# A two-layer decoder trunk on one core: later weight spreads, row pools opened amid the gate tiles, seven banks

## The chip, the cores and the metric

The kernel runs on one core of a Trainium2 chip. The time is device microseconds of one execution, and the median of several executions is compared. TensorE (PE) does the matmuls, VectorE (DVE), ScalarE (ACT) and GpSimd (POOL) the elementwise work, and SyncE (SP) issues the DMAs in order, so what stands behind a waiting DMA in SP's queue waits too.

## The reference

The program is a trunk of two layers on 1024 tokens of 1024 columns, all in float32. Each layer is a token mixer with a gate, an output projection, a DeepNorm layer norm, and a gated addition of a projected side input:

```python
# layer 0, mixer A: three dilated groups, merged by softmax denominators
h = x @ w_in
for gi, (window, dil) in enumerate(A_GROUPS):          # (128,1) (512,4) (2048,16)
    q, k, v = ...; q, k = apply_rope(q), apply_rope(k)
    o, lse = banded_attention(strided(q), strided(k), strided(v), window // dil)
o = sum_g softmax_g(lse) * o_g
mix = (o * silu(z)) @ w_out                            # z: the last 1024 columns of h
# layer 1, mixer B: 16 query heads on 2 key/value heads, window 128, one sink logit per head
o, _ = banded_attention(q, k, v, B_WINDOW - 1, sinks)
mix = (o * silu(z)) @ w_out
# after each mixer
x = layer_norm(alpha * x + mix)
x = x + sigmoid(x @ Wg_i) * (p[i] @ Wp_i)
```

## The kernel before

The tokens lie in eight row tiles of 128. Weights are taken in blocks of 512 output columns (2 MB of float32, 33 blocks in all). Each block and each activation is split into a float16 pair, hi and lo, and one tile times one block (`lin`, lines 270 to 272) is 24 matmuls of 128x512: hi by hi, hi by lo and lo by hi for eight slices of the inner dimension. One PSUM bank holds the result.

**A weight block** passes ten steps of a generator (class `Block`): four row-max reduces on VectorE (`wpm`, line 108), a 128x128 diagonal of the maxima on VectorE (`mdd`, line 228), which one matmul with a matrix of ones (`s<-mdd,ones`, line 235, "the spread") brings to all partitions so that VectorE can make a power of two of the largest; then four split steps (lines 131 and 132: ACT makes hi, VectorE lo). The raw block lies in one of two buffers (`wraw`); block i + 2 is loaded once block i is split, by four DMAs on SP's queue (line 102). A split waits until the block that held its slot is released. `progress` and `prepare` advance this generator by a number of steps per tile of `lin` work: `W_STEPS` 1.6 in general.

**Layer A**: for two halves of the heads and three groups, a value block and two query/key blocks with rope; the attention is worked off in units (scores, mask and max on VectorE, exps on ACT, a hi/lo split, a transposing DMA to `pT`, value matmuls, `st` to `scr` in DRAM), a few units behind the `lin` tiles. A merge reads `scr` as `gt` and writes `oa`. **Layer B**: a block of keys and values, two query blocks, and units that end in `mu`, stored to `ob`.

**The gate and the rows**: two blocks of gate columns. `z_tile` makes silu of one tile (`zt`, `zu`) and stores it to `za` or `zb`. `rows(n)` loads a merged row tile (`ot`) and its gate (`og`), multiplies them on POOL, splits them and transposes them to `ogT`. `norm(n)` multiplies `ogT` by the two output blocks ("whl" and "wo"), adds the residual row on VectorE (`y`, line 920), takes the statistics (line 921), a reciprocal square root (POOL's pow, line 1003), normalizes (line 927) and transposes `xgT`. `gate` multiplies `xgT` by the two side-gate blocks ("whl" and "wg"), with tanh on ACT. Where code of several stages is open, a scheduler orders each engine's instructions; the pools below set which memory is free when.

Before, `z_block` runs all of gate half 0 and one tile of half 1, then `drain` finishes every attention unit and merge; only then are the pools of the rows (`tp`, `pw`) opened. `mixed` then does the other seven tiles of half 1 with five weight steps each, and `rows` for the last four tiles of these; the other four rows are made within norm.

Of the kernel before, what the change touches and what calls it, by code (L numbers as in the profile page):

```python
# [20 lines left out]
P = 128  # L21
S = 1024
D = 1024
# [57 lines left out]
W_OP = 2  # L81
N_WAKE = 8
Z_AHEAD = 1
ROWS_AHEAD = 4
# [4 lines left out]
class Block:  # L89
# [6 lines left out]
    def load(self):  # L96
        k = self.k
        self.n = NK * self.cols
        self.raw = k.raw.tile([P, NK * 512], F32, tag="wraw", name="wraw")
        q = self.n // 4  # L100
        for c in range(4):
            k.nc.sync.dma_start(self.raw[:, c * q:(c + 1) * q], self.src[:, c * q:(c + 1) * q])

    def maxima(self):
# [7 lines left out]
        yield True  # L112
        e = k.max_spread(diag)
# [25 lines left out]
class Trunk:  # L139
    def __init__(self, ctx, tc, a):  # L140
# [13 lines left out]
        self.uid = 0  # L154
# [25 lines left out]
        self.mhalf = self.const.tile([P, 1], F32, name="mhalf")  # L180
        nc.gpsimd.memset(self.mhalf, -0.5)
# [7 lines left out]
    def rope_tables(self, order):  # L189

        t = self.const.tile([P, N_ROPE], F32, name="rope", tag="rope", bufs=2)
# [124 lines left out]
    def drain(self):  # L316
        due, self.due = self.due, []
        for e in due:
            e[1]()
        while self.units or any(self.pipe):  # L320
            self.unit_step()
        self.merge_every = 1
        while self.merges or self.merging:
            self.merge_step()

# [9 lines left out]
    def rope_out(self, ps, nq, nk, n, dst):  # L335
# [6 lines left out]
        t2 = w.tile([P, 512], F32, tag="t2", name="t2")  # L342
# [8 lines left out]
        hl = w.tile([P, 12, P], F16, tag="hl", name="hl", bufs=3)  # L351
# [18 lines left out]
    def scores(self, qa, kas, mask, cs, ncs, sums, nbias, floor, pool_lo):  # L370
# [31 lines left out]
        nc.sync.dma_start(ptf, pf[:, :8 * nk], transpose=True)  # L402
# [188 lines left out]
    def weight_steps(self):  # L591
# [4 lines left out]
        for i in range(len(b)):  # L596
            yield from b[i].split()
            if i + 2 < len(b):
                b[i + 2].load()
            if i + 1 < len(b):  # L600
                yield from b[i + 1].maxima()

    def next_block(self):
        b = self.blocks[self.bi]
        self.bi += 1
        while not b.done:
            assert next(self.steps)
        return b
# [13 lines left out]
    def layer_a(self):  # L622
# [15 lines left out]
        for pair in range(2):  # L638
            for g in (1, 2, 0):
                if pair and g == 0:  # L640
                    self.merge_every = 1
                self.rope_tables(g)
# [4 lines left out]
                for n in range(NT):  # L647
                    ps = self.ps_lin.tile([P, 512], F32, tag="lin", name="lin")
                    self.lin(ps, blk, *self.stat_a(g, n), 0, 512)
                    self.v_out(ps.rearrange("p (s c) -> p s c", s=2), vh[:, pick, n, :], vl[:, pick, n, :])  # L650
# [19 lines left out]
        self.z_block(self.invx, lambda n: self.stat_a(0, n))  # L670
        self.drain()
# [15 lines left out]
    def unit_a(self, q, g, n, qk, vh, vl, cs, ncs, cv, scr):  # L687
# [4 lines left out]
        def stats():  # L692
            st = at.tile([P, 4 * HD + 8], F32, tag="st", name="st", bufs=len(self.pipe) + 1)
# [21 lines left out]
    def z_rows(self, pool, ps, c):  # L715
# [4 lines left out]
        u = pool.tile([P, 512], F32, tag="t2", name="zu")  # L720
# [4 lines left out]
    def z_tile(self, pool, n, half):  # L725
        ps = self.ps_lin.tile([P, 512], F32, tag="lin", name="lin")
        self.lin(ps, self.w_z, *self.z_stat(n), 0, 512)
        self.nc.sync.dma_start(self.z_dr[n][:, 512 * half:512 * half + 512], self.z_rows(pool, ps, self.cz))

    def z_block(self, invx, stat):  # L730

        self.z_stat = stat
        self.upt = 2.0
        for half in range(2):
            self.w_z = self.next_block()
            self.cz = self.prod(invx, self.w_z.inv, 0.5, "cz")
            for n in range(Z_AHEAD if half else NT):
                self.z_tile(self.work, n, half)
                self.progress()
            if half == 0:  # L740
                self.w_z.released = True

    def merge(self, n, pair, scr):

        nc, at, sp = self.nc, self.att, self.small
# [44 lines left out]
    def layer_b(self, xT, invx):  # L790
# [4 lines left out]
        self.bufs = 3  # L795
        self.rope_tables(0)
# [7 lines left out]
        for n in range(NT):  # L804
# [4 lines left out]
            self.progress()  # L809
# [23 lines left out]
        self.z_block(invx, lambda n: self.stat_t(xT, n))  # L833
        self.drain()
# [35 lines left out]
    def transpose_rows(self, src, s, dst, i, name):  # L870
# [6 lines left out]
        nc.sync.dma_start(t.rearrange("p a k c -> p (a k) c"), hl.rearrange("p a c -> p (a c)"), transpose=True)  # L877
        dst[i] = t

    def mixed(self, l, xres, gate_pool):  # L880
# [4 lines left out]
        g_b = pw.tile([P, D], F32, tag="g_b", name="g_b", bufs=1)  # L885
        b_b = pw.tile([P, D], F32, tag="b_b", name="b_b", bufs=1)
        nc.sync.dma_start(g_b, a["lng"][l].partition_broadcast(P))
        nc.sync.dma_start(b_b, a["lnb"][l].partition_broadcast(P))
# [3 lines left out]
        w_o, cw = [], []  # L892
# [17 lines left out]
        def norm(n):  # L910
            y = pw.tile([P, D], F32, tag="row", name="y", bufs=6)
            nc.sync.dma_start(y, xres(n))
            sc = sp.tile([P, 2], F32, tag="osc", name="osc")
            st = sp.tile([P, 2, 6], F32, tag="bst", name="bst")
            for hf in range(2):
                sl = slice(512 * hf, 512 * hf + 512)
                nc.vector.tensor_mul(sc[:, hf:hf + 1], ris[n], cw[hf])
                ps = self.ps_lin.tile([P, 512], F32, tag="lin", name="lin")
# [13 lines left out]

        done = 0
        for n in range(Z_AHEAD, NT):
            self.z_tile(self.work, n, 1)
            self.tick()
            self.prepare(5)
            if n >= NT - ROWS_AHEAD:
                rows(done)
                done += 1  # L940
        self.w_z.released = True
        for i in range(2):
            b = self.next_block()
            c = self.keep(1, "cw")
            nc.vector.tensor_scalar(c, b.inv, 1.0 / ALPHA, None, op0=ALU.mult)
            w_o.append(b)
            cw.append(c)
        for n in range(NT):
# [4 lines left out]
            if n == 1:  # L953
                wg = gate_pool()
        for b in w_o:
            b.released = True
        return xgT, xg_dr, wg

    def gate(self, l, xgT, xg_dr, last):
# [8 lines left out]
        for n in range(NT):  # L968
# [5 lines left out]
            for c0, c1 in ((0, 512), (512, 768), (768, 1024)) if end else ((0, 512), (512, 1024)):  # L974
                hf, sl, w = c0 // 512, slice(c0, c1), c1 - c0
                ps = self.ps_lin.tile([P, 512], F32, tag="lin", name="lin")[:, :w]
                self.lin(ps, w_g[hf], *self.stat_t(xgT, n), c0 % 512, w)
                t = pw.tile([P, 512], F32, tag=("g_b", "b_b")[hf], name="gth", bufs=1)[:, :w]
# [168 lines left out]
```

## Time and profile before

| | us |
|---|---|
| median of 3 runs (1661.18 to 1664.79) | 1662.65 |
| the profiled execution | 1663.47 |
| its span | 1661.6 |
| TensorE busy | 1587.1 |
| VectorE busy | 1082.3 |
| ScalarE busy | 923.1 |
| GpSimd busy | 673.5 |

By the trace, layer A's attention ends near 975 us, its second gate half begins near 1006, norm near 1047 and the side gate near 1128; layer B's attention lasts from about 1277 to 1462, its norm begins at 1490. A busy time is a mean over all of these stages; where TensorE was idle or ran at a lower clock is read stage by stage.

### The profile page before, as it was taken

The page shows a single profiled execution, that of the slowest core. Times are in us where ns is not written, and L with a number is a line of the kernel's source. Part 1 is how long each engine was busy: PE and PEld are TensorE (multiplying, and loading weights), DVE is VectorE, ACT ScalarE, POOL GpSimd, SP SyncE. Part 2 cuts the span into 40 slices and gives each one's busy share as a digit, 9 for nine tenths or more (in the row PEclk, how much of TensorE's full clock was granted, in tenths as well). Part 3 has the DMA queues.
Part 4 walks back from the last instruction along what each step waited for, and adds up shares of the span by engine and source line. Part 5 has one row for each costly group of instructions (what it writes and reads, how often), then busy time and mean ns, then how long its engine had stood idle before and what let it go on. Part 6 is the DMA issues. An engine that isn't in the chain of part 4 may idle for free. (4 is left out here: it accounts for less than half of the span.)

```text
span 1661.6 us, 29030 instructions
## 1 busy us (share of the span) xinstructions
PE 1587.1 (96%) x10579; PEld 882.0 (53%) x10579; DVE 1082.3 (65%) x2617; ACT 923.1 (56%) x2050; POOL 673.5 (41%) x481
## 2 busy tenths in 40 slices
PE   9899999999999799999999988889999998999998
PEld 3455676654555456766555543334455555544444
DVE  6756665655666876556566567877347988678731
ACT  4526665674765477656657843533334888754321
POOL 0205524432564666154235553452323552225331
PEclk9999999999999899999999999999999999999999
DMA  9617766774887777567558996989975898998963
GB/s 364 247 61 162 169 157 137 159 166 112 160 166 203 212 166 157 133 152 162 143 127 183 187 232 218 329 216 261 250 183 110 160 206 171 189 299 215 260 197 107
DMA packets 543792, 311.02 MB, mean 187 GB/s; under 512 B 473120, under 2 KB 494240, under 8 KB 543392
## 3 DMA queue, kind: packets, MB, share of 16 engines
q1 hardware_dynamic: 543648, 309.16, 75.2%
q8 instruction: 83, 1.36, 0.3%
q14 instruction: 61, 0.50, 0.1%
HBM read 137.78 MB, written 54.92 MB: 116 GB/s over the span
## 5 line engine op out<-in xcount | busy, mean ns | idle before, releaser
L270 PE MATMUL lin<-whl,xhl 128*128 128x512 f16 x1280 | 488.5, 382 | 0.0
L272 PE MATMUL lin<-whl,xhl 128*128 128x512 f16 x1280 | 488.3, 382 | 0.0
L271 PE MATMUL lin<-whl,xhl 128*128 128x512 f16 x1280 | 488.0, 381 | 0.0
L399 POOL TENSOR_TENSOR phl<-sm,phl 128x1024 f16<-128x1024 f32 (+1 forms) x88 | 155.6, 1768 | 233.7 <-ACT phl L397 212.9
L349 POOL TENSOR_TENSOR t<-t,t 128x512 f32<-128x512 f32 (+1 forms) x120 | 153.4, 1278 | 235.5 <-DVE t L348 219.0
L108 DVE TENSOR_REDUCE wpm<-wraw 128x1 f32<-128x1024 f32 (+1 forms) x132 | 157.1, 1198 | 99.3 <-DMA wraw<-in_wa_dram 59.1
L272 PEld LDWEIGHTS <-xhl 128*128 128x128 f16 x1280 | 149.3, 117 | 127.1 <-issue 3.2
L270 PEld LDWEIGHTS <-xhl 128*128 128x128 f16 x1280 | 149.3, 117 | 119.0 <-issue 2.8
L271 PEld LDWEIGHTS <-xhl 128*128 128x128 f16 x1280 | 149.7, 117 | 116.6 <-issue 3.3
L393 ACT ACTIVATE sm<-sm,st,cs 128x128 f32<-128x128 f32 (+1 forms) x384 | 203.6, 532 | 3.3
L356 POOL TENSOR_TENSOR hl<-t,hl 128x512 f16<-128x512 f32 (+1 forms) x120 | 143.5, 1196 | 133.4 <-ACT hl L355 133.4
L387 DVE CUSTOM_DVE_ANT_0 sm<-s,tab 128x256 f32<-128x256 f32 (+1 forms) x512 | 157.1, 358 | 34.3 <-PE s L383 25.8
L132 DVE SCALAR_TENSOR_TENSOR whl<-wraw,s,whl 128x1024 f16<-128x1024 f32 (+1 forms) x116 | 168.6, 1504 | 10.9 <-ACT whl L131 10.9
L355 ACT ACTIVATE hl<-t 128x512 f16<-128x512 f32 (+1 forms) x120 | 72.3, 602 | 123.1 <-POOL t L349 121.6
L345 DVE TENSOR_TENSOR t<-lin,rope 128x512 f32<-128x512 f32 (+1 forms) x120 | 78.9, 658 | 84.3 <-PE lin L272 59.7
L131 ACT ACTIVATE whl<-wraw,s 128x1024 f16<-128x1024 f32 (+1 forms) x116 | 121.8, 1123 | 7.0 <-DVE s L210 7.0
L271 PE MATMUL lin<-whl,x2T 128*128 128x512 f16 (+1 forms) x320 | 115.0, 359 | 0.0
L270 PE MATMUL lin<-whl,x2T 128*128 128x512 f16 (+1 forms) x320 | 115.0, 359 | 0.0
L272 PE MATMUL lin<-whl,x2T 128*128 128x512 f16 (+1 forms) x320 | 115.0, 359 | 0.0
L397 ACT ACTIVATE phl<-sm 128x1024 f16<-128x1024 f32 (+1 forms) x128 | 110.2, 861 | 1.2
L359 ACT ACTIVATE hl<-hl 128x512 f16<-128x512 f16 (+1 forms) x104 | 63.2, 608 | 54.2 <-POOL hl L356 54.0
L383 PE MATMUL s<-qk 128*128 128x128 f16 x1120 | 81.8, 221 | 8.1 <-DMA qk<-hl 8.1
(190 smaller groups left out, 2897.3 us busy)
## 6 DMA issues: line engine op xcount, KB each, us to landing
wraw<-in_wa_dram SPq DMA_DIRECT2D x56, 512.0 KB, 5.8
scr<-st SPq DMA_DIRECT2D x96, 132.0 KB, 2.3
gt<-scr SPq DMA_DIRECT2D x48, 264.0 KB, 3.4
wraw<-in_wav_dram SPq DMA_DIRECT2D x24, 512.0 KB, 6.1
prh<-pro SPq DMA_DIRECT2D x32, 256.0 KB, 4.6
wraw<-in_wg_dram SPq DMA_DIRECT2D x16, 512.0 KB, 8.8
wraw<-in_wb_dram SPq DMA_DIRECT2D x16, 512.0 KB, 6.5
xg<-y SPq DMA_DIRECT2D x16, 512.0 KB, 3.5
```

Source lines behind the costliest of these rows:

```text
L108: k.nc.vector.tensor_reduce(pm[:, c:c + 1], self.raw[:, c * q:(c + 1) * q], axis=AX.X, op=ALU.max, apply_absolute_value=True)
L131: nc.scalar.activation(hl[:, 0, sl], self.raw[:, sl], AF.Copy, scale=self.s)
L132: nc.vector.scalar_tensor_tensor(hl[:, 1, sl], self.raw[:, sl], self.s, hl[:, 0, sl], op0=ALU.mult, op1=ALU.subtract)
L270: mm(ps, xh(kt), wh, start=(kt == 0), stop=False)
L271: mm(ps, xh(kt), wl, start=False, stop=False)
L272: mm(ps, xl(kt), wh, start=False, stop=(kt == NK - 1))
L349: nc.gpsimd.tensor_add(t1[:, :nh * HD], t1[:, :nh * HD], t2[:, :nh * HD])
L356: nc.gpsimd.tensor_sub(hl[:, :nh, HD:P], rv, hl[:, :nh, 0:HD])
L387: nc.vector.tensor_tensor_reduce(sm[:, h, :nk], ps[:, i, :nk], mask, 1.0, -3e38, ALU.add, ALU.max, mx[:, h:h + 1])
L393: nc.scalar.activation(sm[:, h, :nk], sm[:, h, :nk], AF.Exp, bias=nbias[:, h:h + 1], scale=cs, accum_out=sums[:, h:h + 1])
L397: nc.scalar.activation(hl[:, 0], sm[:, :, :nk], AF.Copy)
L399: eng.tensor_sub(hl[:, 1], sm[:, :, :nk], hl[:, 0])
```

## The change

- A spread step of a block in the gate tiles, norm and side gate (`late`) waits until two tiles of `lin` work are done since its diagonal (`SPREAD`). `next_block` takes the remaining steps at once if a block is due.
- In those stages a block's load is issued after the latest transposing DMA (`moved`), and block i + 2 is loaded after the second row-max reduce of block i + 1, not right after the split of block i.
- Gate tiles advance three weight steps each (`W_GATE`), where they had 1.6 in half 0 and 5 in half 1; keys of layer B advance 0.8.
- `drain` is gone: the attention pools close, and the pools of the rows open, within gate half 0 as soon as no unit is left (`leave`). Merges have a pool of their own.
- `rows` follows two tiles behind in gate half 1: six of the eight rows are there, two in norm.
- `bank` takes turns among seven PSUM banks (four were for scores alone) for gate half 1, norm and the side gate.
- The layer norm's `g_b` and `b_b` are loaded at norm's start from a pool of that stage; a gate store is issued one tile later; there is one rope table instead of two, loaded at the third value tile; `t2` has three buffers.
- The reciprocal square root is ACT's square root and VectorE's reciprocal; the two `osc` products are one.

```diff
+    def load(self):
+        k = self.k
+        with k.tc.issue_after(k.moved.ins) if k.late and k.moved else nullcontext():
+            self.transfers()
 ...
         diag = k.max_diag(pm)
         yield True
+        at = k.work_done + SPREAD
+        while k.work_done < at and k.late:
+            yield False
         e = k.max_spread(diag)
 ...
             yield from b[i].split()
-            if i + 2 < len(b):
-                b[i + 2].load()
+            new = b[i + 2:i + 3]
+            if new and not self.late:
+                new.pop().load()
+            count = 0
             if i + 1 < len(b):
-                yield from b[i + 1].maxima()
+                for did in b[i + 1].maxima():
+                    count += did
+                    if new and count == 2:
+                        new.pop().load()
+                    yield did
 ...
+    def bank(self):
+        self.turn += 1
+        pool, tag = ((self.ps_s, "s"), (self.ps_lin, "lin"))[self.turn % 7 % 2]
+        return pool.tile([P, 512], F32, tag=tag, name=tag)
 ...
+    def gate_tiles(self, leave):
+        self.upt = 2.0
+        self.late = True
+        self.z_block(0)
+        for n in range(NT):
+            self.z_tile(self.work, n, 0)
+            self.progress(W_GATE)
+            if leave and not (self.due or self.units or any(self.pipe)):
+                leave()
+                leave = None
 ...
-            self.progress()
+            self.progress(W_STEPS / 2)          # keys of layer B
 ...
-        for n in range(Z_AHEAD, NT):
+        for n in range(NT):
             self.z_tile(self.work, n, 1)
             self.tick()
-            self.prepare(5)
-            if n >= NT - ROWS_AHEAD:
+            self.prepare(W_GATE)
+            if n >= ROW_LAG:
                 rows(done)
                 done += 1
 ...
-        nc.gpsimd.tensor_tensor(r, v, self.mhalf, op=ALU.pow)
+        nc.scalar.activation(r, v, AF.Sqrt)
+        nc.vector.reciprocal(r, r)
 ...
+        self.gate_tiles(lambda: row_pools([att], [("tp", 9), ("pw", 2)]))
+        xgT, xg_dr, gp = self.mixed(0, lambda n: a["x"][n * P:(n + 1) * P, :], lambda: gate_pool("wg"))
```

The change moves instructions on every engine from about 952 us on. On SP's queue at the end of layer A's attention, where the last units' transposes are issued (`qk` for scores, `pT` for values), the order before is:

```order
L360 DMA_TRANSPOSE qk<-hl 128x12x128
L748 DMA gt<-scr_1_620 128x528
L102 DMA wraw<-in_ao_dram 128x1024 x3
L706 DMA scr_1_620<-st 128x264
L360 DMA_TRANSPOSE qk<-hl 128x12x128
L402 DMA_TRANSPOSE pT<-phl 128x16x128
L728 DMA za_609<-zu 128x512
```

In the changed program the load of the same block stands here:

```order
L722 DMA scr_1_621<-st 128x264
L408 DMA_TRANSPOSE pT<-phl 128x16x128
L108 DMA wraw<-in_ao_dram 128x1024 x4
L799 DMA oa_604<-gt 128x2x256
L748 DMA za_613<-zu 128x512
L722 DMA scr_1_621<-st 128x264
```

The three DMAs of the raw output block stood ahead of the last `qk` transpose; now all four stand behind the last `pT`.

On TensorE around the spread of the second side-gate block, "wg" (`ones` is the matrix of ones, `xhl` the input, `ogT` the gated rows, `xgT` the normed rows), the order before is:

```order
L272 LDWEIGHTS xhl_106
L272 MATMUL lin_11974<-whl_11083,xhl_106 128x512
L235 LDWEIGHTS ones_80
L235 MATMUL s_12294<-mdd_12292,ones_80 128x128
L270 LDWEIGHTS ogT_11868
L270 MATMUL lin_12035<-whl_11616,ogT_11868 128x512
```

and in the changed program:

```order
L282 LDWEIGHTS ogT_12276
L282 MATMUL lin_12732<-wo_11905,ogT_12276 128x512
L245 LDWEIGHTS ones_80
L245 MATMUL s_12759<-mdd_12651,ones_80 128x128
L280 LDWEIGHTS xgT_12147
L280 MATMUL s_12812<-whl_12310,xgT_12147 128x512
```

It stood between the last gate tile and the first tile of norm; now it stands between the last tile of norm's output and the first tile of the side gate.

On SP's queue at the end of layer B's attention, where the last results (`ob`) are stored and the first row loads follow, the order before is:

```order
L863 DMA ob_13430<-mu 128x256
L728 DMA zb_13433<-zu 128x512
L863 DMA ob_13430<-mu 128x256
L887 DMA g_b<-in_lng_dram 128x1024
L888 DMA b_b<-in_lnb_dram 128x1024
L897 DMA ot<-ob_13423 128x1024
L898 DMA og<-zb_13431 128x1024
L897 DMA ot<-ob_13424 128x1024
L898 DMA og<-zb_13432 128x1024
```

and in the changed program:

```order
L748 DMA zb_13434<-zu 128x512
L892 DMA ob_13431<-mu 128x256
L748 DMA zb_13435<-zu 128x512
L892 DMA ob_13431<-mu 128x256
L922 DMA ot<-ob_13424 128x1024
L923 DMA og<-zb_13432 128x1024
L922 DMA ot<-ob_13425 128x1024
L923 DMA og<-zb_13433 128x1024
L922 DMA ot<-ob_13426 128x1024
```

The loads of `g_b` and `b_b` stood ahead of the first `ot`; now the row loads follow the last `ob` at once.

More of the change, by code (lines that the diff above doesn't have):

```diff
@@ L1 @@
 import math
-from contextlib import ExitStack
+from contextlib import ExitStack, nullcontext
 import numpy as np
@@ L153, in __init__ @@
         self.o_i = 0
-        self.uid = 0
+        self.moved = None
+        self.uid = self.turn = 0
+        self.z_out = None
+        self.late = False
         self.bufs = 2
@@ L725, in z_tile, with z_block @@
     def z_tile(self, pool, n, half):
-        ps = self.ps_lin.tile([P, 512], F32, tag="lin", name="lin")
+        ps = self.bank() if half else self.ps_lin.tile([P, 512], F32, tag="lin", name="lin")
         self.lin(ps, self.w_z, *self.z_stat(n), 0, 512)
-        self.nc.sync.dma_start(self.z_dr[n][:, 512 * half:512 * half + 512], self.z_rows(pool, ps, self.cz))
-    def z_block(self, invx, stat):
-        self.z_stat = stat
-        self.upt = 2.0
[L734 to L738, printed above, removed]
-                self.progress()
-            if half == 0:
-                self.w_z.released = True
+        out = self.z_out
+        self.z_out = (self.z_dr[n][:, 512 * half:512 * half + 512], self.z_rows(pool, ps, self.cz))
+        for o in (out, self.z_out if half and n == NT - 1 else None):
+            if o:
+                self.nc.sync.dma_start(*o)
+        if half and n == NT - 1:
+            self.z_out = None
+    def z_block(self, half):
+        invx, self.z_stat = self.z_in
+        self.w_z = self.next_block()
+        self.cz = self.prod(invx, self.w_z.inv, 0.5, "cz")
+    def gate_tiles(self, leave):
+        self.upt = 2.0
+        self.late = True
[6 more added lines that the diff above has]
+                leave = None
+        assert leave is None
+        self.w_z.released = True
     def merge(self, n, pair, scr):
-        nc, at, sp = self.nc, self.att, self.small
+        nc, at, sp = self.nc, self.attm, self.small
         gt = at.tile([P, 3, 2, 4 * HD + 8], F32, tag="gt", name="gt")
@@ L795, in layer_b @@
         self.bufs = 3
+        self.late = False
         self.rope_tables(0)
@@ L916, in norm @@
                 sl = slice(512 * hf, 512 * hf + 512)
[L917 to L918 removed]
+                ps = self.bank()
                 self.lin(ps, w_o[hf], *self.stat_t(ogT, n), 0, 512)
@@ L952, in mixed, with gate @@
                 done += 1
-            if n == 1:
-                wg = gate_pool()
         for b in w_o:
             b.released = True
-        return xgT, xg_dr, wg
-    def gate(self, l, xgT, xg_dr, last):
+        return xgT, xg_dr, gp
+    def gate(self, l, xgT, xg_dr, gp, last):
         nc, a, pw = self.nc, self.a, self.pw
@@ L1049, in build, with row_pools @@
         lower = [xpool]
-        work, self.work = opened("work", 2)
-        lower.append(work)
-        with tc.tile_pool(name="att", bufs=2) as self.att:
-            self.layer_a()
-        tp, self.tp = opened("tp", 9, side="right")
-        pw, self.pw = opened("pw", 2, side="right")
+        for name in ("work", "attm"):
+            p, pool = opened(name, 2)
+            setattr(self, name, pool)
+            lower.append(p)
+        att, self.att = opened("att", 2)
+        self.layer_a()
+        pools = []
+        def row_pools(first, last):
+            for p in first:
+                close(p)
+            for name, bufs in last:
+                p, pool = opened(name, bufs, side="right")
+                setattr(self, name[:2], pool)
+                pools.append(p)
         def gate_pool(name):
```

98 lines of the change are left out of this document (47 added, 51 removed).

## The prediction

> **What bounds the kernel now.** I read the page's first part, then busy time and granted clock by stretches, then what TensorE waited for in the stretches that lose time.
>
> ```profile
> span 1661.6 us, 29030 instructions
> PE 1587.1 (96%) x10579; PEld 882.0 (53%) x10579; DVE 1082.3 (65%) x2617; ACT 923.1 (56%) x2050; POOL 673.5 (41%) x481
> ```
>
> TensorE is busy 96% of the span, so nothing that the other engines save counts unless TensorE was waiting for it. No matmul is added or removed. All that can be won is TensorE's idle time and the time it runs at a lower clock. The stretches (start:end, length, busy time and instructions of PE, PEld, DVE, ACT, POOL, granted clock, DMA share, GB/s):
>
> ```profile
> 0.00:925.00 925.00, 900.03 (x6112) 530.12 (x6113) 581.92 (x1472) 561.80 (x1338) 391.09 (x286) 0.99 0.70 168
> 925.00:975.00 50.00, 43.67 (x389) 24.94 (x387) 33.92 (x94) 39.38 (x96) 27.40 (x19) 0.93 0.95 210
> 1000.00:1175.00 175.00, 153.93 (x686) 67.91 (x684) 136.79 (x268) 68.75 (x85) 72.28 (x44) 0.95 0.87 250
> 1277.00:1418.00 141.00, 127.81 (x1325) 77.80 (x1323) 125.98 (x401) 117.75 (x319) 60.45 (x41) 0.99 0.88 171
> 1462.00:1490.00 28.00, 24.44 (x114) 10.96 (x113) 19.04 (x40) 18.50 (x25) 8.47 (x6) 0.99 0.97 316
> 1490.00:1650.00 160.00, 160.00 (x736) 72.27 (x735) 90.21 (x153) 45.44 (x52) 63.38 (x40) 0.99 0.73 205
> ```
>
> Loss of a stretch is idle time plus busy time times (1 - clock). Until 925 us: 25.0 + 9.0 = 34. From 925 to 975 (end of layer A's attention): 6.3 + 3.1 = 9.4. From 1000 to 1175 (second gate half and norm): 21.1 + 7.7 = 28.8. From 1277 to 1418 (layer B's attention): 13.2 + 1.3 = 14.5. From 1462 to 1490: 3.6 + 0.2, and the low clock just behind it, about 1.6 of the last row's (1 - 0.99) x 160: 5.4. Together 58 us from 925 on. The engine orders of the two programs agree up to about 952 us except for one rope-table load, so the first 34 us stay; 58 us is the ceiling.
>
> What TensorE waited for, from 925 to 1175 and then from 1225 to 1500 us (total, times, longest):
>
> ```profile
> PE s L235 <- DVE mdd L228: 13.6, 2, 7.5
> PE lin L270 <- DMA ogT<-rhl: 4.9, 3, 2.9
> PE o L414 <- DMA pT<-phl: 4.5, 1, 4.5
> PE s L383 <- DMA qk<-hl: 1.8, 1, 1.8
> ...
> PE o L414 <- DVE mu L861: 8.2, 5, 2.7
> PE s L235 <- DVE mdd L228: 3.6, 1, 3.6
> ```
>
> The spread matmul (L235) is TensorE's only part in finding a weight block's scale. It sits in TensorE's queue right behind the diagonal that VectorE makes (L228), and everything of TensorE stands behind it.
>
> **Layer A's end: -6 us.** SP's queue there (start, time, what it issues):
>
> ```profile
> 951.18 1.28 SPq L102 DMA_DIRECT2D wraw<-in_ao_dram  x3
> 952.56 0.38 SPq L706 DMA_DIRECT2D scr<-st  x1
> 953.03 2.88 SPq L360 DMA_TRANSPOSE qk<-hl  x1
> 960.84 1.32 SPq L402 DMA_TRANSPOSE pT<-phl  x1
> ```
>
> The load of a raw weight block waits for its buffer, and the last two transposes of the attention stand behind it; then TensorE waits 4.5 us for pT, 1.8 for qk, and runs at a lower clock. The change issues that load after the last transpose, and VectorE's row-max reduces on it go too. I take 6 of 9.4: the 4.5, and most of the low clock that followed. Bounds: all 9.4, or nothing if the next item in the chain (exps, the split of the probabilities) takes over at once.
>
> **Gate half 1 and norm: -20 us.** The two spreads that cost 13.6 us stood behind diagonals that came late:
>
> ```profile
> 1019.33 1.22 DVE L108 TENSOR_REDUCE wpm<-wraw 128x1 f32<-128x1024 f32 x1 [0.98 <-DMA wraw<-in_wg_dram]
> 1025.40 2.33 DVE L108 TENSOR_REDUCE wpm<-wraw 128x1 f32<-128x1024 f32 x2
> 1029.61 0.29 DVE L228 TENSOR_SCALAR mdd<-tab,mde 128x128 bf16<-128x128 f32 x1
> ```
>
> Merges, gate and weight work share VectorE between 1019 and 1030; TensorE has no other work once it reaches the spread. The change moves each late spread two tiles of TensorE work (48 matmuls) behind its diagonal. How long that is, and what a dip costs:
>
> ```profile
> 1025.00:1050.00 25.00, 18.41 (x73) 7.73 (x73) 17.05 (x38) 12.25 (x18) 8.43 (x6) 0.86 0.83 307
> 1175.00:1200.00 25.00, 25.00 (x118) 11.33 (x116) 9.65 (x10) 7.78 (x10) 7.94 (x7) 1.00 1.07 281
> ```
>
> A full 25 us holds 118 matmuls, 0.212 us each, so 48 are 10.2 us: more than the longest spread wait, 7.5. In the order the wg0 spread stands two tiles into norm, and the wg1 spread right ahead of the gate stage. So 13.6 goes, and the low clock behind those two stalls, which is most of the 7.7. The remaining 7.5 of idle time (ogT rows, y) shrinks: six of eight rows are made in gate half 1 instead of four, so four ogT are ready early; in norm VectorE's work falls, and seven banks instead of three let TensorE run ahead of VectorE's evictions. I leave 3 us of it.
>
> What is new is the end: wg1's split can only start after its spread, which is the last thing ahead of the gate.
>
> ```profile
> L132 DVE SCALAR_TENSOR_TENSOR whl<-wraw,s,whl 128x1024 f16<-128x1024 f32 x112 | 164.3, 1517 | 10.5 <-ACT whl L131 10.5
> L108 DVE TENSOR_REDUCE wpm<-wraw 128x1 f32<-128x1024 f32 x128 | 154.5, 1214 | 99.3 <-DMA wraw<-in_wa_dram 59.1 <-DMA wraw<-in_ao_dram 11.4 <-DMA wraw<-in_wav_dram 11.2
> L132 DVE SCALAR_TENSOR_TENSOR wg<-wraw,s,wg 128x1024 f16<-128x1024 f32 x8 | 13.4, 1697 | 0.0
> L920 DVE SCALAR_TENSOR_TENSOR y<-lin,osc,y 128x512 f32<-128x512 f32 x32 | 23.7, 743 | 10.1 <-DMA y<-in_x_dram 9.4 <-PE lin L272 0.7
> L921 DVE BATCH_NORM_STATS2 bst<-y 128x6 f32<-128x512 f32 x32 | 21.9, 687 | 0.5
> L927 DVE SCALAR_TENSOR_TENSOR y<-y,mv,g_b 128x1024 f32<-128x1024 f32 x16 | 20.4, 1275 | 0.0
> L1003 POOL TENSOR_TENSOR rr<-rv,mhalf 128x1 f32<-128x1 f32 x16 | 22.5, 1404 | 62.2 <-DVE rv L1001 59.2 <-DVE rs L210 3.0
> ```
>
> From the last y on, VectorE has 0.74 + 0.69 + 1.28 + some 0.8 of small steps, then 4 x 1.70 = 6.8 for wg: 10.3 us. TensorE has 38 matmuls ahead of the first that reads wg: 8.1 us. Since that matmul reads only the first quarter, the stall is 0 to 4; I take 2, and 3 for a clock dip and the g_b and b_b loads that now stand ahead of y in norm. Sum: 28.8 - (3 + 2 + 3) = 20.8, rounded to 20. Bounds 10 to 26: below, if the DMA traffic of half 1 decides (a rival); above, if all but the 2 to 3 of wg1 go.
>
> Other edits here cost nothing on the path. POOL's pow, 16 x 1.40 = 22.5 us, leaves POOL; in its place ACT takes a square root and VectorE a reciprocal of one column (an estimate: no more than the 0.29 of the 128x128 mdd row), under 5 us of VectorE over both layers, and 32 osc products become 16. ACT now changes its function table four times more:
>
> ```profile
> L486 ACT ACT_TABLE_LOAD x1 | 1.3, 1283 | 0.7 <-PEq L1136 0.7
> ```
>
> 4 x 1.28 = 5.1 us of ACT, one at the start of each norm and one at each gate start; in layer A's stretch ACT was busy 69 of 175 us. Its next consumers (xgT of the first row, the first tanh) have several tiles of slack. Without that slack it would be 5.1.
>
> **Layer B's attention: +1.5 us.** Here VectorE is the bound: busy 126 of 141.
>
> ```profile
> L132 DVE SCALAR_TENSOR_TENSOR whl<-wraw,s,whl 128x1024 f16<-128x1024 f32 x8 | 13.6, 1745 | 0.0
> L108 DVE TENSOR_REDUCE wpm<-wraw 128x1 f32<-128x1024 f32 x8 | 9.7, 1212 | 4.2 <-DMA wraw<-in_bo_dram 4.2
> ```
>
> The stretch holds two splits and two maxima of blocks. Keys now pace at half the steps, so by VectorE's order one split more (4 x 1.75 = 7.0) and one maxima more (4 x 1.21 = 4.9) fall between the first and the last score. Against it: the first score comes earlier by the four splits that left the keys (5.6 at 1.4 each), and the 4.2 us wait for raw weights goes, as loads go out later but the reduces are further behind. 11.9 - 5.6 - 4.2 = +2.1; I take 1.5, since some of TensorE's waits there are for other things than VectorE. Bounds: +8, if only the wait goes; -6, if the early start counts fully and the extra block lies in VectorE's gaps (15 us of the stretch).
>
> **Layer B's norm start: +3 us.** The chain from the last value unit to the first ogT (SP, POOL, and the landing times of the two ogT transposes from 1455 to 1492 us):
>
> ```profile
> 1464.43 0.33 SPq L887 DMA_DIRECT2D g_b<-in_lng_dram  x1
> 1465.28 0.43 SPq L897 DMA_DIRECT2D ot<-ob  x1
> 1480.80 4.61 SPq L877 DMA_TRANSPOSE ogT<-rhl  x1
> ...
> 1473.08 4.99 POOL L901 TENSOR_TENSOR og<-og,ot 128x512 f32<-128x512 f32 x4 [32.90 <-DMA og<-zb]
> ...
> DMA to landing us min/median/max: 4.4/6.2/8.0
> ```
>
> The last value unit ends at about 1462; its transposed row landed 8.0 us after 1480.8, that is 27 us later. TensorE had 111 matmuls (23.5 us) of gate tiles behind the value unit, and the rest was the wait of 3.6. In the changed order g_b and b_b (1 MB) no longer stand ahead of ot: the chain becomes 23 to 26 us. But 80 matmuls only (17 us) stand between the last value unit and norm, and the row loads still wait for that unit, since their memory is what the attention held. So 6 to 9 us of stall and a clock dip of 1.6 replace the 5.4: +2 to +5, taken as 3. Bounds -4 (rows start earlier than I think) to +8.
>
> **Layer B's gate start: +2**, for the same wg1 wait as above, where nothing was lost before; 0 to 4.
>
> A rule on the clock is weighed here. The row first: a stall of 2.86 us was followed by matmuls 0.43 us apart in place of 0.21, for some 3.4 us.
>
> ```profile
> 1113.19 0.39 PE L270 MATMUL lin<-whl,ogT 128*128 128x512 f16 x1 [2.86 <-DMA ogT<-rhl]
> 1114.26 0.63 PE L271 MATMUL lin<-whl,ogT 128*128 128x512 f16 x1
> ```
>
> I therefore add 1.6 us to stalls of about 3 us or more. The Trainium skill, "TensorE: Matmul & The Clock Gate", Part 1, says that the clock halves after at least one idle window of about 3.4 us; this row shows it after less. By the page's figure taken strictly the stalls of 2 at the gate starts are free of the dip and those of 6 are not, and the sum would be some 1.5 us lower.
>
> **The sum.** -6 - 20 + 1.5 + 3 + 2 = -19.5 us. The profiled execution took 1663.47, 0.82 above the median of the runs, 1662.65. 1663.47 - 19.5 = 1643.97, less 0.82: 1643. As the norm term was rounded down, I name 1642.
>
> **The rivals.**
>
> All stalls of the middle vanish (1627): -8 - 26 - 2 + 0 + 0 = -36. For it: half of the loss hangs on three spreads; seven banks. Against it: wg1's split cannot start before its spread, and layer B's rows cannot start before the last value unit. Chance 0.2.
>
> Transfers become the bound in gate half 1 (1653). Six rows (12 loads of 0.5 MB), eight gate stores of 0.25 MB, a weight block of 2 MB and the last merges (about 4 MB) are some 14 MB in the 41 us of eight tiles, 340 GB/s; the fastest row above shows 316, and 1025 to 1050 had 307. At 310 it takes 45 us, plus the rows' latency of 8: about 9 us of new stalls, which turn -20 into -11. For it: DMA shares of 0.83 to 1.07 in these rows. Against it: ogT are needed only in norm, so late rows there are hidden. Chance 0.2.
>
> Slower (1675): weight loads held behind transposes. SP's queue is in order; a load that now stands behind the latest transpose waits for VectorE and ACT to finish that row. A block needs its load (8 to 9 us), 4.9 of reduces, 6.8 of splits: 20 us. If wo1 and wg1 of both layers come late by half of it and more (4 x 12 = 48 against 36 of best gains) the kernel is slower. It decides from the point at which loads go out less than 20 us, 94 matmuls, before their first matmul. Against it: in the order wg1's load stands six tiles of norm (60 us) ahead. Chance 0.07.
>
> The idle time only moves, from spreads to ogT and wg (1661): VectorE is busy 137 of 175 us in the gate and norm, and what it has to do there hardly changes. But a stretch that is 78% busy has room, so 0.06. A measurement of this kernel can tell 0.2%, 3.3 us.
>
> **How the numbers follow.** Forecast 0.47, its own range 1634 to 1651. With the rivals: faster 0.87, same 0.06, slower 0.07. The range that holds eight of ten reaches from the first rival to the one on transfers and a little beyond: 1625 to 1658.
>
> **What would show it.** Right: no wait of the spread on mdd from 1000 to 1175 us, clock 1.00 there but for one dip, at least 790 of the 826 matmuls that seven full stretches hold, a wait on wg at both gate starts, and in layer B's norm a wait on ogT of 6 to 9 us. Wrong: waits on ogT or y of more than 10 us in norm (transfers), VectorE's waits on raw weights back, or a last value unit of layer B that ends less than 15 us earlier than now (the terms ahead of it give 24.5).

## The result, and the profile after

The changed kernel takes 1681.33 us (median of four runs, 1678.65 to 1685.08), against 1662.13 before. The ratio is 1.0119, with a 95% interval from 1.0103 to 1.0135: slower by 1.2%, where the prediction had 1642 and a range up to 1658. One execution in all that follows, 1693.94 us of the kernel with two weight steps in norm, ran at a lower granted clock (0.94); it is in that run's median and not in its ratio.

The page's first lines of the changed kernel:

```profile
span 1676.9 us, 29035 instructions
PE 1589.5 (95%) x10579; PEld 882.8 (53%) x10579; DVE 1087.5 (65%) x2617; ACT 930.0 (55%) x2070; POOL 663.3 (40%) x464
```

The work is the same; TensorE's waiting grew. Of the 15.3 us between the two spans 12.9 are idle time of TensorE and 2.4 are slower matmuls. Busy time by stretches of the changed kernel (columns as in the prediction: length, PE, PEld, DVE, ACT, POOL, granted clock, DMA share, GB/s):

```profile
925.00:975.00 50.00, 45.33 (x410) 25.82 (x408) 32.04 (x97) 39.75 (x97) 29.56 (x19) 0.97 0.91 193
1000.00:1120.00 120.00, 114.83 (x528) 51.56 (x526) 98.34 (x179) 53.02 (x72) 49.31 (x32) 0.99 0.88 254
1120.00:1160.00 40.00, 23.64 (x93) 9.71 (x91) 28.97 (x57) 13.52 (x15) 7.05 (x4) 0.79 0.76 202
1277.00:1418.00 141.00, 129.61 (x1343) 79.35 (x1342) 127.91 (x383) 116.18 (x313) 63.82 (x39) 0.99 0.84 172
1418.00:1462.00 44.00, 41.87 (x372) 22.41 (x371) 33.08 (x77) 28.25 (x64) 6.40 (x3) 1.00 0.97 231
1462.00:1500.00 38.00, 27.11 (x138) 12.11 (x136) 21.45 (x37) 18.99 (x26) 14.56 (x8) 0.82 0.71 215
1570.00:1610.00 40.00, 33.22 (x147) 14.61 (x146) 24.40 (x43) 15.92 (x18) 8.65 (x5) 0.91 0.68 180
```

By the prediction's own reckoning (idle time plus busy time at the lower clock), the loss of each stage, in us (the -20 for gate half 1 and norm is taken apart into -22 and the +2 for wg):

| stage | before | after | difference | predicted |
|---|---|---|---|---|
| end of layer A's attention | 9.4 | 6.0 | -3.4 | -6 |
| gate half 1 and norm of layer A | 28.8 | 6.3 | -22.5 | -22 |
| start of layer A's side gate (1120 to 1160) | in the row above | 21.3 | +21.3 | +2 |
| layer B's keys and attention (0.9 + 14.5; 0.6 + 12.7 + 2.1) | 15.4 | 15.4 | 0.0 | +1.5 |
| norm start of layer B | 5.4 | 15.8 | +10.4 | +3 |
| start of layer B's side gate (1570 to 1610) | 0 | 9.8 | +9.8 | +2 |

The sum is +15.6; the two spans differ by 15.3. The stalls at the spreads went, and three new ones took more than they gave. TensorE's waits over the whole execution (total, times, longest), those of layer A's gate and norm, layer B's norm and the attention:

```profile
PE lin L280 <- ACT wg L140: 19.0, 2, 12.2
PE o L420 <- DVE mu L890: 12.6, 10, 3.1
PE s L280 <- DMA ogT<-rhl: 10.9, 1, 10.9
PE s L280 <- ACT ot L928: 5.2, 1, 5.2
PE s L280 <- DVE y L945: 4.2, 1, 4.2
```

**The gate starts.** The timelines of TensorE, VectorE and SP of the changed kernel at layer A's gate start (start, duration; in brackets the idle time before, and what ended it):

```profile
1127.59 0.22 PE L245 MATMUL s<-mdd,ones 128*128 128x128 bf16 x1
1153.97 0.58 PE L280 MATMUL lin<-wg,xgT 128*128 128x512 f16 x1 [12.21 <-ACT wg L140]
...
1127.87 1.43 DVE L114 TENSOR_REDUCE wpm<-wraw 128x1 f32<-128x512 f32 x2 [5.58 <-DMA wraw<-in_wbkv_dram]
1149.73 1.28 DVE L272 SCALAR_TENSOR_TENSOR rhl<-y,lns,rhl 128x1024 f16<-128x1024 f32 x1 [3.47 <-ACT rhl L271]
1151.59 0.28 DVE L247 TENSOR_REDUCE m<-s 128x1 f32<-128x128 f32 x1
...
1120.61 3.36 SPq L906 DMA_TRANSPOSE xgT<-rhl  x1
1124.03 2.01 SPq L108 DMA_DIRECT2D wraw<-in_wbkv_dram  x4
```

TensorE ran the spread of wg at 1127.59. VectorE read its result only at 1151.59, 24 us later, and ACT could begin to split wg only then. From there the first matmul of wg was 2.4 us away (1153.97): of the 26.4 us between the spread and that matmul, 24 are VectorE's lag. The rows of norm stood in VectorE's queue, with two waits of 3.4 and 3.5 us for ACT's half of a row's split (`rhl`), and so did the reduce of a raw block that SP had issued behind two transposes. In layer B, without the raw block:

```profile
1580.58 0.22 PE L245 MATMUL s<-mdd,ones 128*128 128x128 bf16 x1
...
1591.31 1.28 DVE L272 SCALAR_TENSOR_TENSOR rhl<-y,lns,rhl 128x1024 f16<-128x1024 f32 x1 [3.47 <-ACT rhl L271]
1593.17 0.28 DVE L247 TENSOR_REDUCE m<-s 128x1 f32<-128x128 f32 x1
```

The reduce comes 12.6 us after the spread.

**Layer B's norm start.** POOL, VectorE and SP from the row loads to the first ogT:

```profile
1469.56 0.32 SPq L922 DMA_DIRECT2D ot<-ob  x1
...
1474.42 11.79 POOL L926 TENSOR_TENSOR og<-og,ot 128x512 f32<-128x512 f32 x6 [32.16 <-DVE m L247]
...
1476.30 8.79 DVE L141 SCALAR_TENSOR_TENSOR wo<-wraw,s,wo 128x1024 f16<-128x1024 f32 x4
1485.02 0.14 DVE L211 TENSOR_SCALAR p2t<-rm 128x1 f32<-128x1 f32 x1
...
1490.67 4.38 SPq L906 DMA_TRANSPOSE ogT<-rhl  x2
```

The split of the output block wo, late by the spread's delay, stands in VectorE's queue ahead of the scale (`p2t`) of the first row, for 8.8 us.

### The profile page after: what moved, and what is told of

Same layout as the page of the kernel before. It is cut to its first block, busy times and chain, and to the rows that moved or that the text cites. A ratio compares the mean times of both kernels' runs of the same rounds, so it can differ in the third digit from the quotient of the medians.

```text
span 1676.9 us, 29035 instructions
## 1 busy us (share of the span) xinstructions
PE 1589.5 (95%) x10579; PEld 882.8 (53%) x10579; DVE 1087.5 (65%) x2617; ACT 930.0 (55%) x2070; POOL 663.3 (40%) x464
## 5 line engine op out<-in xcount | busy, mean ns | idle before, releaser
L280 PE MATMUL lin<-whl,xhl 128*128 128x512 f16 x1248 | 475.0, 381 | 0.0
L281 PE MATMUL lin<-whl,xhl 128*128 128x512 f16 x1248 | 474.8, 380 | 0.0
L282 PE MATMUL lin<-whl,xhl 128*128 128x512 f16 x1248 | 474.8, 380 | 0.0
L393 DVE CUSTOM_DVE_ANT_0 sm<-s,tab 128x256 f32<-128x256 f32 (+1 forms) x512 | 157.0, 358 | 36.2 <-PE s L389 27.8
L280 PE MATMUL lin<-whl,x2T 128*128 128x512 f16 (+1 forms) x280 | 99.8, 356 | 0.6 <-DVE t L354 0.6
L281 PE MATMUL lin<-whl,x2T 128*128 128x512 f16 (+1 forms) x280 | 99.8, 356 | 0.0
L282 PE MATMUL lin<-whl,x2T 128*128 128x512 f16 (+1 forms) x280 | 99.7, 356 | 0.0
```

Source lines behind the costliest of these rows:

```text
L280: mm(ps, xh(kt), wh, start=(kt == 0), stop=False)
L281: mm(ps, xh(kt), wl, start=False, stop=False)
L282: mm(ps, xl(kt), wh, start=False, stop=(kt == NK - 1))
L393: nc.vector.tensor_tensor_reduce(sm[:, h, :nk], ps[:, i, :nk], mask, 1.0, -3e38, ALU.add, ALU.max, mx[:, h:h + 1])
```

## The experiments

Each run is the changed kernel but for the edit shown, and each computes the whole reference. A ratio is to the kernel before, run beside it on the same chip. A difference in us is one of medians; whether it is clear of noise is read from the intervals of the ratios (the changed kernel: 1.0103 to 1.0135).

### Two weight steps per half tile of norm

The change also halved the weight steps per half tile of norm (`W_OP`, 2 before), which its list doesn't name.

```diff
-W_OP = 1
+W_OP = 2
```

> The changed kernel with two weight steps per half tile of norm, as before the change, in place of one. Theory A (pace): in the changed kernel the second side-gate block is split only once the gate stage is due, because norm's 16 steps don't reach it; with two steps its spread stands 145 to 169 matmuls (31 to 36 us) ahead of its first matmul in place of 38. Expected: the waits on wg (12.2 and 6.8 us) and the low clock behind them go, 22 to 27 us less, about 1656. Theory B (the load of the next stage's block, issued behind the xgT transposes, holds VectorE, and all that follows is late): the wait on wg in layer A stays at 8 us or more, and only layer B's goes; about 1672.

1663.10 us, ratio 0.9996 (0.9984 to 1.0007): 18 us less than the changed kernel, and the same as before the change. No wait on wg is left in either layer. TensorE's longest waits now:

```profile
PE s L280 <- DMA ogT<-rhl: 15.1, 2, 10.4
PE s L280 <- DVE m L226: 4.6, 1, 4.6
```

Theory A holds: with the pace undone the stalls at both gate starts go, though the time came out 7 us above its figure. VectorE still lags, by 22.7 us in layer A (24 in the changed kernel):

```profile
1098.44 0.22 PE L245 MATMUL s<-mdd,ones 128*128 128x128 bf16 x1
...
1121.14 0.28 DVE L247 TENSOR_REDUCE m<-s 128x1 f32<-128x128 f32 x1
```

and by 11.6 us in layer B. But the spread now stands 168 matmuls (some 36 us) ahead of the first that reads wg, in both layers, and they cover the lag. The new 4.6 us lies in layer A's side gate, where VectorE waited for the next raw block:

```profile
1184.14 1.22 DVE L114 TENSOR_REDUCE wpm<-wraw 128x1 f32<-128x1024 f32 x1 [4.86 <-DMA wraw<-in_wb_dram]
```

### Loads not tied behind transposes

```diff
-        with k.tc.issue_after(k.moved.ins) if k.late and k.moved else nullcontext():
+        with nullcontext():
```

> The changed kernel with its late loads no longer tied behind the latest transpose. Theory A: the wait on y before the gate stage of layer A (4.2 us) goes or shrinks, as VectorE no longer waits 5.6 us for raw weights, but the waits on wg stay near 7 us in both layers: 3 to 9 us less, 1672 to 1678. Theory B: the wait on wg in layer A falls under 3 us and the time by 15 us or more, to about 1664.

1686.84 us, ratio 1.0141 (1.0121 to 1.0162): 5.5 us more than the changed kernel, with intervals that overlap. Both theories had it faster; it isn't. The end of layer A's attention, by the same row as above:

```profile
925.00:975.00 50.00, 42.31 (x374) 24.03 (x373) 34.20 (x96) 36.78 (x89) 28.59 (x19) 0.93 0.97 206
```

Its loss is 7.7 + 3.0 = 10.7, 4.7 more than with the tie. That bears out the prediction's first term in kind: with three DMAs of the load ahead of the last `qk` transpose again, TensorE's wait for pT there is 4.6 us, where it is 0.9 with the tie. In norm VectorE's waits for the keys' raw block fell from 6.8 to 2.5 us, but TensorE waited 7.1 us for VectorE there (`rr`) and 9.6 for wg. What makes the `rr` wait isn't settled.

### The same, untied in norm and the side gate alone

```diff
-        with k.tc.issue_after(k.moved.ins) if k.late and k.moved else nullcontext():
+        with k.tc.issue_after(k.moved.ins) if k.tied and k.late and k.moved else nullcontext():
...
-        self.late = True
+        self.late = self.tied = True
...
+        self.tied = False
```

The flag is set at the start of the gate tiles and cleared at the start of norm.

> The changed kernel, its one weight step per half tile of norm kept, with loads tied behind transposes only up to the end of gate half 1. The raw block of layer B's keys then goes out before the first xgT transpose, not behind the third and fourth; the wg spread stays 37 matmuls ahead of its first matmul, as in the changed kernel. Theory C: of layer A's gate start (4.2 us on y, 12.2 on wg) the raw load makes the 4.2 and about 5 of the 12.2 (VectorE waited 6.8 us for it), and the pace the rest: wait on wg 6 to 8 us in both layers, 9 to 13 us less than the changed kernel, 1668 to 1672. Rival A: the pace alone makes the wg wait: it stays above 10 us, 4 to 5 us less, about 1677. Rival B: the raw load makes nearly all in layer A: the wait on wg there under 3 us, 1665.

1678.49 us, ratio 1.0100 (1.0076 to 1.0124), 2.8 less, with intervals that overlap. The wait on y (4.2) is gone, and the one on wg in layer A is not shorter but longer:

```profile
PE lin L280 <- ACT wg L140: 21.7, 2, 14.0
```

VectorE's waits from 1100 to 1170 us in this run:

```profile
DVE rhl L272 <- ACT rhl L271: 9.8, 3, 3.5
DVE wpm L114 <- DMA wraw<-in_wb_dram: 1.8, 2, 1.5
```

Rival A holds: the raw load was worth the wait on y at most. Without it VectorE still reads the result of the wg spread 19.6 us after TensorE made it (1129.96 and 1149.60).

### No delay of the spread

```diff
-SPREAD = 2.0
+SPREAD = 0.0
```

> The changed kernel with no delay of the spread behind its diagonal. Theory A: without the delay a block passes its ten steps sooner, and the spread of wg stands 169 matmuls ahead of its first use: the waits on wg go (24 us with their low clock), and waits of TensorE on mdd come back, 13.6 + 3.6 us with their low clock at the most if the diagonals are as late as in the kernel before, near 0 if the diagonals are early: 1657 to 1677, by the middle 1666. Theory B: the waits on wg stay at half or more, 1672 to 1690.

1673.57 us, ratio 1.0068 (1.0049 to 1.0086), 7.8 less. The waits on wg are gone here too, with one step per half tile: pace and delay together make the wg split late. Other waits come instead:

```profile
PE s L280 <- DMA ogT<-rhl: 21.5, 2, 11.9
PE s L245 <- DVE mdd L238: 14.7, 2, 9.7
```

(5.0 us of the last row lie at the program's start in every kernel.) Where they lie matters:

```profile
1050.18 0.58 PE L280 MATMUL s<-whl,ogT 128*128 128x512 f16 x1 [11.93 <-DMA ogT<-rhl]
1170.31 0.29 PE L245 MATMUL s<-mdd,ones 128*128 128x128 bf16 x1 [9.71 <-DVE mdd L238]
```

The stalled spread is one in the side gate, where the kernel before had no such stall. The two of 13.6 us in gate half 1 and norm of layer A, and the one of 3.6 in layer B, don't come back without the delay; so the other parts of the change remove them without it. Which of these does it (fewer steps per gate tile, the banks, the order of the rows) wasn't taken apart, but with three banks, below, two spreads in norm stall by 7.1 and 3.4 us in spite of the delay. The wait of 11.9 us on ogT stands ahead of layer A's norm, and there the split of wo is in the first row's way:

```profile
1034.42 6.89 DVE L141 SCALAR_TENSOR_TENSOR wo<-wraw,s,wo 128x1024 f16<-128x1024 f32 x4
1041.23 0.14 DVE L211 TENSOR_SCALAR p2t<-rm 128x1 f32<-128x1 f32 x1
```

In the changed kernel that split comes behind the first two rows (1045.38), and TensorE waits 5.2 us there. In layer B it is the other way round: without the delay the split of wo came before the first row's maximum was there, at VectorE's full pace:

```profile
1473.26 4.87 DVE L141 SCALAR_TENSOR_TENSOR wo<-wraw,s,wo 128x1024 f16<-128x1024 f32 x4 [3.14 <-ACT wo L140]
```

So the delay took the split out of the first row's chain in layer A and put it into the one in layer B.

### Layer B's keys at the full pace

```diff
-            self.progress(W_STEPS / 2)
+            self.progress()
```

> The changed kernel with 1.6 weight steps per tile of layer B's keys, as before the change. The prediction put the slower pace at +1.5 us in the attention bound by VectorE. If that holds, the time falls by 1 to 4 us and TensorE's waits on mu (12.6 us) go back to some 8; if the earlier start of the scores is worth more, it rises by up to 5 us.

1677.15 us, ratio 1.0086 (1.0067 to 1.0106), 4.2 less, with intervals that just touch. The waits on mu fell from 12.6:

```profile
PE o L420 <- DVE mu L890: 5.6, 5, 1.9
```

The time fell by as much as was expected at most, but hardly in the attention: by the reckoning of the table the loss of layer B's keys and attention goes from 15.5 to 14.2 us (1225 to 1464 us), as waits on pT and on the keys' tiles grew. The larger part is the norm start, where the wait on ogT fell from 10.9 to 7.1 because 95 matmuls in place of 82 stand behind the last value unit.

### Three banks

```diff
-        pool, tag = ((self.ps_s, "s"), (self.ps_lin, "lin"))[self.turn % 7 % 2]
+        pool, tag = self.ps_lin, "lin"
```

with two weight steps per half tile of norm, as in all the runs that follow down to the last.

> The changed kernel with two weight steps per half tile of norm, with three PSUM banks in place of seven in gate half 1, norm and the side gate. The prediction said that seven let TensorE run ahead of VectorE's evictions. If so, three cost 5 to 15 us, 1668 to 1678, with waits of TensorE's first matmul of a tile on y, zu or gth; if the waits are for data that comes late in any case, no more than 2 us, 1661 to 1665.

1685.60 us, ratio 1.0147 (1.0127 to 1.0167): 22 us slower than with seven banks. TensorE waits for evictions and, behind them, for the diagonals:

```profile
PE s L245 <- DVE mdd L238: 15.4, 3, 7.1
PE lin L280 <- DVE y L945: 13.9, 4, 7.4
```

VectorE reads the result of the wg spread 2.4 us (layer A) and 0.3 us (layer B) after TensorE made it, in place of 22.7 and 11.6 with seven banks, though the spread stands earlier in the order here (288 matmuls ahead of wg's first). So it is the seven banks that let TensorE run ahead. They are worth more than any other part that was tried alone.

### Loads untied in norm and the side gate, with two steps

> The changed kernel with two weight steps per half tile of norm, and with its loads tied behind the latest transpose only up to the end of gate half 1, not in norm and the side gate. Theory: with two steps, what still costs in norm and the side gate of layer A is raw weights that go out behind a transpose, for which VectorE waits with TensorE's evictions queued behind it: 4.6 and 1.9 us of idle time and 3 of low clock. Expected: these go, 6 to 9 us less than with two steps alone, about 1656. Rival: untying in all stages cost the changed kernel 5 us, because an early load takes its place ahead of transposes that TensorE needs sooner; then it is 1663 to 1668 here too.

1661.07 us, ratio 0.9994 (0.9981 to 1.0008), against 0.9996 with two steps alone: the intervals lie over each other. The 4.6 us wait is gone from the profile, but the time shows no gain.

### Three attention units per gate tile

```diff
-        self.upt = 2.0
+        self.upt = 3.0
```

> The changed kernel with two weight steps per half tile of norm, and attention units worked off at three per gate tile in place of two. Theory for the stall of 10.4 us ahead of layer B's norm: it is the chain from the last value unit to the first ogT (28 us in the changed kernel) less the matmuls that stand between them (82, 17.4 us). Here 90 stand between them (19.1 us), and by VectorE's order the first row's scale comes ahead of the split of wo, which took 8.8 us: chain 23 to 25, stall 4 to 6, the time 5 to 8 us less than with two steps alone, about 1657. Rival: the chain is set by the row loads and POOL alone and the order on VectorE doesn't matter; then the stall falls by the 1.7 us of the eight matmuls only, about 1661.

1656.14 us, ratio 0.9971 (0.9958 to 0.9985), 7 us less than with two steps alone (0.9984 to 1.0007, so the intervals just touch). The wait ahead of layer B's norm fell from 10.4 to 7.5, not to 4 to 6: the scale of the first row came ahead of wo's split, but its lo half (`rhl`) still stood behind it.

### Two weight steps per gate tile

```diff
-W_GATE = 3
+W_GATE = 2
```

> The changed kernel with two weight steps per half tile of norm, and two in place of three per gate tile. By VectorE's order the first two rows of layer B are then split ahead of the split of wo, with 81 matmuls (17.2 us) behind the last value unit. Theory (wo's split stands in the chain): the chain falls to 22 to 24 us, as in the run without the spread's delay (22.5), and the stall to 5 to 7; wo, now split later, may cost up to 4 us. The time: 3 to 6 us less than with two steps alone, or the same if wo is late. Rival (loads and POOL set the chain): the stall stays near 10, no change or slower by up to 6.

1657.06 us, ratio 0.9965 (0.9951 to 0.9978), 6 us less. Here scale and split of the first row stand ahead of wo, and the longest wait on ogT is 4.3:

```profile
PE s L280 <- DMA ogT<-rhl: 8.0, 2, 4.3
```

The runs agree on one sum. The matmuls behind the last value unit (counted in TensorE's order) at the prediction's 0.212 us each, plus the wait on ogT, give the chain from that unit to the first ogT (the times in the traces give the same to 0.2 us):

| run | matmuls | their time | wait | chain |
|---|---|---|---|---|
| changed kernel | 82 | 17.4 | 10.9 | 28.3 |
| two steps in norm | 82 | 17.4 | 10.4 | 27.8 |
| three units | 90 | 19.1 | 7.5 | 26.6 |
| keys at full pace | 95 | 20.1 | 7.1 | 27.2 |
| no delay of the spread | 62 | 13.1 | 9.6 | 22.7 |
| two steps per gate tile | 81 | 17.2 | 4.3 | 21.5 |

Where wo's split stands in the chain it is 26.6 to 28.3 us, where it doesn't it is 21.5 to 22.7: the split costs some 5 us there.

### The edits together

```diff
-W_OP = 1
-W_GATE = 3
+W_OP = 2
+W_GATE = 2
...
-        self.upt = 2.0
+        self.upt = 3.0
```

> The changed kernel with two weight steps per half tile of norm, two per gate tile, and three attention units per gate tile: the two edits that each took 5 to 6 us together. Theory (the stall ahead of layer B's norm is the chain of the first row less the matmuls behind the last value unit): 94 matmuls (19.9 us) and a chain of 21.5, as with two steps per gate tile (4.3 + 17.2): stall 1 to 3, where the single edits left 4.3 and 7.5. The time 1651 to 1655. Rival: the gain of each is the same one and doesn't add: 1656.

Two steps per gate tile, two per half tile of norm and three units: 1649.19 us, ratio 0.9935 (0.9917 to 0.9953). By the medians the gains add, 12 us below the kernel before, but the interval touches that of two steps per gate tile alone (0.9951 to 0.9978), so the rival isn't excluded. The profiled execution took 8 us more than the median; in it the wait ahead of layer B's norm is 2.4 us, where 1 to 3 was expected.

> The same with loads tied behind transposes only up to the end of gate half 1. Theory: 0 to 3 us less than the same without it, as it took 2 us from the kernel with two steps alone (1661.07 against 1663.10), 1649 to 1654. Rival: that difference was noise, and it stays within 1 us.

With the loads untied in norm and the side gate: 1656.41 us, ratio 0.9976 (0.9964 to 0.9989). This is slower than without that edit, where 0 to 3 us less was expected. Its profile has a wait on ogT of 5.6 us in the middle of layer B's norm, which the profile without the edit doesn't have; what makes it, and whether it is the difference, wasn't tried.

> The first of these with 1.6 weight steps per tile of layer B's keys. 126 matmuls (26.7 us) stand behind the last value unit, and a chain of 22 to 24: no stall ahead of layer B's norm, and 2 to 4 us less in the attention, as that edit took 4.2 us from the changed kernel: 1647 to 1652. Rival: the slower keys were worth their price and the gain in the changed kernel came from the norm start alone; then it is within 1 us of the first.

With the keys at full pace: 1647.07 us, ratio 0.9918 (0.9903 to 0.9933), the fastest of all, 0.8% under the kernel before; its interval overlaps that of the first. 126 matmuls (26.7 us) cover the chain, and the waits from 1455 to 1500 us are:

```profile
PE lin L280 <- ACT wo L140: 2.0, 1, 2.0
PE lin L281 <- DVE wo L141: 0.9, 1, 0.9
```

No wait on ogT is left there, as the sum said; wo, split later now, costs 3 us.

```diff
-        nc.scalar.activation(r, v, AF.Sqrt)
-        nc.vector.reciprocal(r, r)
+        nc.gpsimd.tensor_tensor(r, v, self.mhalf, op=ALU.pow)
```

> The first of these with the reciprocal square root by POOL's pow (1.40 us a row) as before the change, so with one table load on ACT in place of five. The prediction put this edit at nothing on the path: within 2 us of the first. Rival: ACT's square root in VectorE's order makes VectorE wait for ACT, and pow is 3 to 8 us faster; or pow stands in POOL's queue ahead of the rows and is 3 to 8 us slower.

With the reciprocal square root on POOL again, and the keys at half pace: 1653.18 us, ratio 0.9953 (0.9938 to 0.9967), against 0.9935 (0.9917 to 0.9953) with ACT's square root. The intervals overlap. That POOL is 3 to 8 us faster is ruled out; that it is slower by some us is not.

## Why the prediction was wrong

**Gate half 1 and norm: right in size, and in part by luck.** The spreads' waits went, and the loss fell to 6.3 where 6 was left. But the prediction gave the 13.6 us to the delay of the spread, and without the delay none of these stalls comes back. The run with three banks shows that the gain rests on the banks; the delay kept wo's split out of layer A's first row, which the prediction didn't say.

**The gate starts: the step that failed.** The prediction summed VectorE's work "from the last y on" to 10.3 us, set 38 matmuls (8.1 us) against it, and took a stall of 2. It let VectorE start with TensorE, so it put the lag between the two at nothing. VectorE read the spread's result 12.6 us (layer B) and 24 us (layer A) after TensorE made it. The prediction named the cause itself, as a gain: seven banks let TensorE run ahead of VectorE's evictions. With them the matmuls ahead of wg are done while VectorE is still at earlier rows; with three banks the lag is 0.3 and 2.4 us. The two terms were 2 each and measured 21.3 and 9.8; twice as many weight steps in norm took 18 us away.

**Fewer steps in norm were not priced at all.** The edit of W_OP is what put the wg spread last, 38 matmuls ahead of its use; with two steps it stands 168 ahead in both layers. The order showed the place; the prediction took the place as given and asked only for the length of the chain behind it.

**Layer B's norm start: right in kind, mis-sized.** Stall and cause were forecast as 6 to 9 us with a dip of 1.6, and measured 10.9 and, by the matmuls' own starts, 2.4 (4.9 by the reckoning of the table). The chain was taken as 27 less g_b and b_b; it is 28.3, because wo's split came into it. The prediction looked for what left the chain, not for what the later spreads brought in.

**The end of layer A's attention: right in kind, too large.** 3.4 in place of 6; without the tie it is 4.7 worse.

**Layer B's attention: about 0 in place of +1.5**, within its bounds. The two runs that undo the keys' slower pace took 4.2 us less than the changed kernel, and 2.1 less together with the other edits, where the intervals overlap. Most of the 4.2 came from the norm start, so a cost in the attention itself isn't shown.

**The rivals.** The slower case named raw loads behind transposes, late by 12 us and more in four places. The tie did cost the 4.2 us wait on y, and no more that shows. The transfers did not become the bound in half 1. The nearest was the last one, with a chance of 0.06: it said that the idle time would move from the spreads to ogT and wg because VectorE's work there hardly changes. It moved there, but the rival had the sum unchanged (1661) and not 15 us longer. No rival had the whole mechanism: a block whose split begins only when an engine that lags has got to it.

**The signs.** The wait on wg at both gate starts and the end of the spreads' stalls were named as signs of being right, and came. From 1000 to 1175 us, though, the clock was 0.94 and 690 matmuls ran, where at least 790 were to; VectorE's waits on raw weights were back (6.8 us); and layer B's last value unit ended at 1467 us, 5 later than before and not 24.5 earlier. Its place in the order had also moved, with 82 matmuls behind it in place of 111, which is 6 us that the 24.5 left out.

## What to carry to other kernels

A stall is the length of a chain less the work that covers it, and both must start at the same time: read in the trace how far the engine that begins the chain lags behind the one that waits, and add that lag. Whatever lets one engine run ahead (here, more banks) shortens the cover of everything that the lagging engine has yet to make, so it wants its weights prepared earlier, not later. When a step is delayed to take it out of one wait, look up which chain it lands in, and run the kernel without the delay: a wait that stays away didn't need it.

## What the runs showed of the hardware

VectorE and POOL slowed each other. In the changed kernel four split steps of wo took 8.79 us while POOL multiplied rows (six halves in 11.79 us, 1.97 each; in the kernel before, four that ran while VectorE did no split took 4.99, 1.25 each); in the run without the spread's delay the same four took 4.87, the last 1.1 us of it beside POOL. The Trainium skill, "GPSIMD Engine Reference", section "Key points", says that POOL shares its SBUF interfaces with VectorE and that VectorE's instructions with two SBUF inputs contend there; the split step has two, and this trace agrees.

The low clock behind a long stall cost less than the table's reckoning says. Matmuls of 128x512 start 0.216 us apart at full clock; from their starts, those behind the three long stalls (12.2 with 4.2 ahead of it, 10.9 and 6.8 us) lost 3.9, 2.4 and 1.7 us, where 1.6 had been added for a dip. The granted clock of a stretch counts idle time too: 0.82 over the 38 us of layer B's norm start is 6.8 us of clock, most of it while TensorE waited anyway. So the reckoning gives 5.0, 4.9 and 3.0.
